# A bidirectional gated DeltaNet layer: the scan's ACT row is written anew, and the branch products between its steps are dealt out anew

## The chip, the cores and the metric

The kernel runs on one core of one Trainium2 chip. The metric is the device time of one execution in microseconds (us). The engines are named as in the profile: PE (TensorE, the matrix products), PEld (its weight loads), DVE (VectorE), ACT (ScalarE), POOL (GpSimd) and SP (SyncE, here only an issuer of DMAs). Each engine works through its own instructions strictly in order.

## The reference

One layer works on 2048 latent tokens and 256 context tokens of width 1024. It projects the normalised input, then runs two branches: A, a gated DeltaNet scan in both directions with eight heads of width 128, and B, a gated short convolution. Each branch is projected, gated, added, projected again, and a residual LayerNorm ends it. What matters here is the scan of branch A, cut to its core:

```python
def _gdn_chunked(q, k, v, g, beta, s0):
    g_cum = jnp.cumsum(g.reshape(b, h, n, CHUNK), axis=-1)
    decay = jnp.exp(jnp.where(tri_incl, g_cum[..., :, None] - g_cum[..., None, :], -jnp.inf))
    m = jnp.where(tri_strict, jnp.einsum('bhncd,bhnsd->bhncs', k_beta, k) * decay, 0.0)
    t_inv = lax.linalg.triangular_solve(eye + m, eye, left_side=True, lower=True)
    qk = jnp.einsum('bhncd,bhnsd->bhncs', q, k) * decay
    ...
    def step(s, xs):
        v_new = u_i - jnp.einsum('bhck,bhkv->bhcv', w_i, s)
        o = jnp.einsum('bhck,bhkv->bhcv', q_dec_i, s) + jnp.einsum('bhcs,bhsv->bhcv', qk_i, v_new)
        s = s * d_i[..., None, None] + jnp.einsum('bhck,bhcv->bhkv', k_dec_i, v_new)
        return s, o
```

## The kernel before

Three stages follow each other: the projections (to about 1860 us of the span), the scan in the function `window` (to about 2960 us), and `final` with the output projection and LayerNorm.

The scan treats chunks of 128 tokens. There are 18 chunks and two directions, so 36 visits, the directions by turns. One turn of the loop `for i in range(-3, nv)` works on several visits at once: `v0` runs its state step, `v1` finishes the triangular inverse, `v2` gets its product of queries and keys and the first, serial part of its inverse, and `v3` gets its decays and its product of keys and keys. The order of the lines in the loop is the order of each engine's row (`manual_schedule`). Nothing reorders it, so an instruction that waits holds all that stand behind it on its engine.

The names are these. `gcb` holds the decays: DVE forms eight differences (L143), ACT takes the exponential (L146), DVE multiplies by beta (L150). `gram` is the product on PE (L168) that becomes `N` (keys by keys) or `QK` (queries by keys) by a DVE product with `gcb` (L173). On a chunk's first visit ACT also copies the raw product to a tile (L171) and writes it to memory (L172, `kkd` for N and `kqd` for QK), and DVE's product waits for that copy. On the second visit, from the other direction, the raw product is loaded and only multiplied (L162). The first visits of the 16 latent chunks are called the first half here and their second visits the second half.

The inverse begins with `inv_base`, a generator that the loop advances with `go(sol, n)`. Four ACT copies take N's diagonal blocks (L182, `n32`), one more halves them (L186, `n16`), then DVE runs 15 row steps (`L200`, `L207`, `L210`: a shuffle into `rb`, a product and an addition into `R`), ACT spreads the result (L214, `r32`) and DVE transposes it (L217, `r32t`). The small products of `inv_w16` (L229, copied by ACT at L232) and `inv_d16` (L241, taken up by DVE at L243 and L245), and their like for 32 and 64 rows (L269, L283 to L285, L296 with the ACT copy `w64` at L299, L310) double the inverse's blocks. The large result `R` is laid out by ACT at L303 and completed at L311.

The state step is `st_ks` (PE L322, DVE L324), `st_v` (PE L331, ACT copy L334), `st_o` (PE L342 and L343) and `st_u` (PE L350, DVE L355). POOL scales keys (`kt`, L119) and queries (`qd`, L148).

Between these steps `dense(n)` puts n products of 128x512 of the branch projections on PE (L1286, L1288, L1290; "fillers" below). 24 of them make one tile, which DVE takes up at L1229 (`gt`). What the scan does not take runs at the head of `final`. The norms of finished chunks (`norm`, ACT L1497 and L1507, a chain of twelve tiny DVE steps) run only in the second half. The raw-product tile is named `zat` and has two buffers, and `norm` uses the same two:

```python
            if v["latent"]:
                kc = self.g1.tile([P, 4, P], F32, name="zat", bufs=2)
                nc.scalar.copy(out=kc, in_=kk)
                nc.scalar.dma_start(keep[:, hs], kc)
            nc.vector.tensor_tensor(out=N[:, hs], in0=kk, in1=v["gcb"][:, hs], op=ALU.mult)
```

Of the kernel before, what the change touches and what calls it, by code (L numbers as in the profile page):

```python
# [15 lines left out]
P = 128  # L16
# [21 lines left out]
class Kern:  # L38
# [118 lines left out]
    def gram(self, v, name, rhs):  # L157
# [6 lines left out]
        for g in range(2):  # L164
            hs = slice(4 * g, 4 * g + 4)
            kk = self.pg.tile([P, 4, P], F32, name="gram")
            for h in range(4 * g, 4 * g + 4):
                nc.tensor.matmul(kk[:, h - 4 * g, :], kT[:, h, :], rhs[:, h, :], start=True, stop=True)  # L168
            if v["latent"]:
                kc = self.g1.tile([P, 4, P], F32, name="zat", bufs=2)  # L170
                nc.scalar.copy(out=kc, in_=kk)  # L171
                nc.scalar.dma_start(keep[:, hs], kc)  # L172
            nc.vector.tensor_tensor(out=N[:, hs], in0=kk, in1=v["gcb"][:, hs], op=ALU.mult)  # L173
# [117 lines left out]
    def inv_w64(self, v):  # L291
# [6 lines left out]
        with self.tc.high_priority(100):  # L298
            nc.scalar.copy(out=v["w64"][p2], in_=wp[p2])  # L299
        v["R"] = R = self.g2.tile([P, H, P], F32, name="R")  # L300
# [890 lines left out]
    def window(self, es, settle):  # L1191
# [153 lines left out]
        with tc.manual_schedule(engines={ET.PE, ET.DVE, ET.Activation, ET.Pool, ET.SP}):  # L1345
# [22 lines left out]
            for i in range(-3, nv):  # L1368
# [4 lines left out]
                if i < -1:  # L1373
                    dense(FILL(i) // 2)
# [6 lines left out]
                go(sol, 2)  # L1381
                go(norms)
                if v1:
                    self.visit_load2(v1)
                    self.inv_w16(v1)

                if v2 and v2["latent"]:
                    self.gram(v2, "QK", v2["qT"])
                if i == -1 or v2 and v2["again"] or not v2:
                    dense(8)  # L1390
# [8 lines left out]
                go(sol)  # L1399
# [3 lines left out]
                go(sol)  # L1403
# [4 lines left out]
                if i >= -1:  # L1408
                    dense(4)
# [5 lines left out]
                if v0:  # L1415
                    self.st_u(v0, 0)
                if v1:
# [14 lines left out]
                if i >= -1:  # L1432
# [9 lines left out]
                go(dec)  # L1442
                if i >= -1:
                    dense(8)
                if v1:
                    self.inv_w64(v1)
                go(norms)
                go(sol, 9)
                go(dec)
                if i < -1:  # L1450
                    dense(FILL(i) - FILL(i) // 2)

                if v3:
                    self.gram(v3, "N", v3["kT"])
                    sol = self.inv_base(v3)
                if i == -1 or v3 and v3["again"] or not v3:
                    dense(8)
                ship()
                if v1:
                    self.inv_d64(v1)  # L1460
                go(sol, 2)
                go(norms)
                if i == -1 or not v3 or not v3["again"]:
                    dense(8)
# [281 lines left out]
```

## Time and profile before

| what | value |
|---|---|
| time, median of 3 runs (lowest, highest) | 3278.37 us (3275.57, 3281.44) |
| the profiled execution: its time, its span | 3288.09 us, 3286.4 us |
| busy share of PE, DVE, ACT, POOL over the span | 90%, 67%, 46%, 43% |
| mean granted clock of TensorE | 0.952 |
| first share of the chain that ended last | DVE 19%, PE 9%, DMA 6% |

The shares are means over stages with different limits. In the projections PE is busy nearly throughout. In the scan no engine is, and what ends the waits there has to be read visit by visit.

### The profile page before, as it was taken

To read this page: it belongs to the slowest core of one execution; us is meant where nothing else is said; L and a number is where in the kernel's file an instruction comes from. 1 tells how busy PE (TensorE), PEld (TensorE's weight loads), DVE (VectorE), ACT (ScalarE), POOL (GpSimd) and SP (SyncE) were. 2 spreads that over 40 slices of the span, in tenths; PEclk is the share of its full clock that TensorE was granted. 3 is DMA by queue.
4 is the path that set the end of the run, shared out by engine and by line. 5 is a ranking of instruction groups with operands and counts; after the bars stand their busy time and mean duration, and the time that the engine had idled before them with its cause. 6 is when DMAs were issued, how large, how long until landed. Compare 5 with 4: busy or idle time off the path is not lost. (4 is left out here: it accounts for less than half of the span.)

```text
span 3286.4 us, 60301 instructions
## 1 busy us (share of the span) xinstructions
PE 2963.1 (90%) x22089; PEld 2436.8 (74%) x22089; DVE 2212.4 (67%) x5658; ACT 1517.6 (46%) x3405; POOL 1401.0 (43%) x1021
## 2 busy tenths in 40 slices
PE   7899899999998899999999778899998688887887
PEld 3678668888886777888888667788887577775676
DVE  7756746565656574565732268887889799966499
ACT  4664644333446645333334145555555556552121
POOL 3443447766567554666666111111111222225264
PEclk9999999999999999999999989999998788898999
DMA  5533763324565433222233565575676668677742
GB/s 209 150 103 100 230 207 106 93 84 127 175 190 160 118 95 87 77 78 87 87 114 103 205 235 200 213 264 213 248 265 228 233 223 299 204 235 247 252 140 100
DMA packets 405380, 557.23 MB, mean 170 GB/s; under 512 B 28244, under 2 KB 278613, under 8 KB 404060
## 3 DMA queue, kind: packets, MB, share of 16 engines
q1 hardware_dynamic: 382158, 520.77, 48.7%
q10 hardware_dynamic: 22926, 32.62, 2.7%
q8 instruction: 173, 2.83, 0.3%
q14 instruction: 123, 1.01, 0.1%
HBM read 391.66 MB, written 161.64 MB: 168 GB/s over the span
## 5 line engine op out<-in xcount | busy, mean ns | idle before, releaser
L785 PE MATMUL pd<-bh,ah 128*128 128x512 f32 x2240 | 890.9, 398 | 10.4 <-ACT u L805 5.8
L787 PE MATMUL pd<-bh,al 128*128 128x512 f32 x2240 | 879.3, 393 | 0.0
L786 PE MATMUL pd<-bl,ah 128*128 128x512 f32 x2240 | 878.7, 392 | 0.0
L369 POOL TENSOR_TENSOR al<-s,ah 128x512 fp32r<-128x512 f32 x348 | 478.5, 1379 | 468.6 <-ACT ah L368 396.0
L369 POOL TENSOR_TENSOR al<-raw,ah 128x512 fp32r<-128x512 f32 x260 | 370.8, 1430 | 323.4 <-ACT ah L368 291.2
L785 PEld LDWEIGHTS pd<-bh,ah 128*128 128x128 f32 x2240 | 424.5, 190 | 99.4 <-issue 6.6
L787 PEld LDWEIGHTS pd<-bh,al 128*128 128x128 f32 x2240 | 424.2, 189 | 91.0 <-POOL al L369 0.2
L786 PEld LDWEIGHTS pd<-bl,ah 128*128 128x128 f32 x2240 | 424.5, 190 | 85.4
L368 ACT CAST ah<-s 128x512 fp32r<-128x512 f32 x352 | 214.3, 618 | 290.2 <-PE pd L786 262.8
L119 POOL TENSOR_TENSOR kt<-kt,kd 128x1024 f32<-128x1024 f32 x36 | 71.1, 1976 | 522.4 <-DMA kt<-kd 356.6
L368 ACT CAST ah<-raw 128x512 fp32r<-128x512 f32 x264 | 162.3, 616 | 263.1 <-PE pd L786 171.6
L1286 PE MATMUL pf<-ah,wh 128*128 128x512 f32 x512 | 219.1, 428 | 48.5 <-DMA wh<-w_bhd 21.9
L771 DVE TENSOR_TENSOR s<-s,raw 128x512 f32<-128x512 f32 x80 | 109.4, 1368 | 220.1 <-POOL s L771 220.1
L1290 PE MATMUL pf<-ah,wl 128*128 128x512 f32 x512 | 221.4, 432 | 20.0 <-DMA wl<-w_ald 17.4
L1288 PE MATMUL pf<-al,wh 128*128 128x512 f32 x512 | 216.4, 423 | 0.6 <-POOL al L369 0.6
L148 POOL TENSOR_TENSOR qd<-qd,qT 128x1024 f32<-128x1024 f32 x32 | 75.8, 2368 | 244.5 <-ACT qd L139 173.8
L207 DVE TENSOR_TENSOR rb<-rb,R 128x120 f32<-128x120 f32 (+4 forms) x540 | 165.2, 306 | 14.2
L210 DVE TENSOR_TENSOR R<-R,rb 128x120 f32<-128x120 f32 (+4 forms) x540 | 159.7, 296 | 1.2
L1286 PEld LDWEIGHTS pf<-ah,wh 128*128 128x128 f32 x512 | 103.9, 203 | 73.6 <-issue 34.9
L1290 PEld LDWEIGHTS pf<-ah,wl 128*128 128x128 f32 x512 | 103.9, 203 | 48.1 <-DMA wl<-w_ald 22.9
L1047 ACT ACTIVATE t<-t 128x512 f32<-128x512 f32 (+1 forms) x112 | 67.2, 600 | 141.2 <-DVE t L1032 141.1
L342 PE MATMUL pst<-S,qd 128*128 128x128 f32 x512 | 105.4, 288 | 17.5 <-ACT v L334 9.6
(349 smaller groups left out, 5911.1 us busy)
## 6 DMA issues: line engine op xcount, KB each, us to landing
raw<-in_w_in SPq DMA_DIRECT2D x160, 512.0 KB, 3.8
kT<-kTd SPq DMA_DIRECT2D x36, 512.0 KB, 9.0
gcb<-gcd SPq DMA_DIRECT2D x36, 512.0 KB, 6.0
kt<-kd SPq DMA_DIRECT2D x36, 512.0 KB, 7.1
vh<-vd SPq DMA_DIRECT2D x36, 512.0 KB, 8.4
wh<-w_bhd SPq DMA_DIRECT2D x32, 512.0 KB, 4.2
wl<-w_bld SPq DMA_DIRECT2D x32, 512.0 KB, 5.6
qT<-qTd SPq DMA_DIRECT2D x32, 512.0 KB, 9.1
```

Of the source, the lines that this page charges most:

```text
L207: nc.vector.tensor_tensor(out=t, in0=t, in1=bc(R[:, :, j:j + 1], c.stop - c.start), op=ALU.mult)
L210: nc.vector.tensor_tensor(out=R[:, :, c], in0=R[:, :, c], in1=t, op=ALU.add)
L342: nc.tensor.matmul(po[:, j, :], v["qd"][:, h, :], S[:, h, :], start=True, stop=False)
L368: self.nc.scalar.copy(out=hi, in_=src)
L369: (eng or self.nc.gpsimd).tensor_tensor(out=lo, in0=src, in1=hi.bitcast(F32), op=ALU.subtract)
L771: eng.tensor_tensor(out=o, in0=a, in1=b, op=op)
L785: mm(ps, hi[:, k, :], bh, start=(first and k == 0), stop=False, skip_group_check=not first)
L786: mm(ps, hi[:, k, :], bl, start=False, stop=False, skip_group_check=not first)
L787: mm(ps, lo[:, k, :], bh, start=False, stop=(last and k == 3), skip_group_check=not first)
L1286: mm(ps, wh[:, k, :], ah, start=(k == 0), stop=False)
L1288: mm(ps, wh[:, k, :], al, start=False, stop=False)
L1290: mm(ps, wl[:, k, :], ah, start=False, stop=(k == KT - 1))
```

## The change

Four things are done, all in the scan. The raw-product tile gets a name of its own, `kc`, with three buffers. The part of `inv_w64` that lays out `R` becomes a function of its own, `inv_x64`, called after N's product. The steps of the decays and of the serial inverse move: the exponential L146 goes behind the `w64` copy, `n32` and `n16` go from the end of a turn to the next turn behind the copies of QK, and more row steps stand after the decays' differences. The fillers are dealt out anew: 24 a turn in the first half and 32 in the second as before, at other places; 24 instead of 40 in the turn i = -1; 32 instead of 40 in the last turns.

```diff
-                kc = self.g1.tile([P, 4, P], F32, name="zat", bufs=2)
+                kc = self.g1.tile([P, 4, P], F32, name="kc", bufs=3)
...
+
+    def inv_x64(self, v):
+        nc = self.nc
         v["R"] = R = self.g2.tile([P, H, P], F32, name="R")
...
-                go(sol, 2)
-                go(norms)
                 if v1:
                     self.visit_load2(v1)
                     self.inv_w16(v1)
+                go(norms)
...
-                if i == -1 or v2 and v2["again"] or not v2:
-                    dense(8)
+                if full:
+                    dense(3 if gram_q else 11)
                 ship()
                 go(sol, 2)
...
-                go(sol)
                 if v0:
                     self.st_v(v0, 0)
                     self.st_v(v0, 1)
-                go(sol)
+                go(sol, 2)
...
-                if i >= -1:
-                    dense(4)
+                if full:
+                    dense(3)
...
-                go(dec)
-                if i >= -1:
-                    dense(8)
+                if full:
+                    dense(8 if gram_n else 6)
                 if v1:
                     self.inv_w64(v1)
+                go(dec)
                 go(norms)
-                go(sol, 9)
+                go(sol, 3)
                 go(dec)
...
                 if v3:
                     self.gram(v3, "N", v3["kT"])
+                if full:
+                    dense(4 if gram_n else 8)
+                ship()
+                go(sol)
+                if v1:
+                    self.inv_x64(v1)
+                    self.inv_d64(v1)
+                go(sol)
+                go(norms)
+                if full and gram_n:
+                    dense(2)
+                if v3:
                     sol = self.inv_base(v3)
-                if i == -1 or v3 and v3["again"] or not v3:
-                    dense(8)
-                ship()
-                if v1:
-                    self.inv_d64(v1)
-                go(sol, 2)
-                go(norms)
-                if i == -1 or not v3 or not v3["again"]:
-                    dense(8)
```

In the changed kernel the line numbers behind L297 are three higher (L303 becomes L306, L324 becomes L327), and behind `window`'s loop seven.

ACT's row around the copies of N in a turn of the first half, before:

```order
L146 ACTIVATE gcb<-gcb 128x1024
L299 COPY w_19036<-pinv 64x512
L303 ACTIVATE R<-r_18854,m64l 128x8x64
L303 ACTIVATE R<-r_18854,m64h 128x8x64
L214 ACTIVATE r_19041<-R_18717,m16l 128x8x16
L214 ACTIVATE r_19041<-R_18717,m16h 128x8x16
L171 COPY zat<-gram 128x512
L172 DMA kkd_181<-zat 128x512
L171 COPY zat<-gram 128x512
L172 DMA kkd_181<-zat 128x512
L311 ACTIVATE R<-pinv 64x8x64
```

The same place of the changed kernel:

```order
L299 COPY w_18976<-pinv 64x512
L146 ACTIVATE gcb<-gcb 128x1024
L171 COPY kc<-gram 128x512
L172 DMA kkd_181<-kc 128x512
L171 COPY kc<-gram 128x512
L172 DMA kkd_181<-kc 128x512
L214 ACTIVATE r_19013<-R_18776,m16l 128x8x16
L214 ACTIVATE r_19013<-R_18776,m16h 128x8x16
L306 ACTIVATE R<-r_18784,m64l 128x8x64
L306 ACTIVATE R<-r_18784,m64h 128x8x64
L314 ACTIVATE R<-pinv 64x8x64
```

The `w64` copy now precedes the exponential, and N's two copies come directly behind the exponential, ahead of `r32` and of `R`.

ACT's row right behind that place, before, to the copies of `st_v`:

```order
L182 ACTIVATE n_19075<-N 32x256 x4
L186 ACTIVATE n_19080<-n_19075,m16l 128x128
L232 COPY w_19165<-pinv 128x256
L171 COPY zat<-gram 128x512
L172 DMA kqd_197<-zat 128x512
L171 COPY zat<-gram 128x512
L172 DMA kqd_197<-zat 128x512
L334 COPY v_19243<-pst 128x512
```

The same place of the changed kernel:

```order
L232 COPY w_19090<-pinv 128x256
L171 COPY kc<-gram 128x512
L172 DMA kqd_197<-kc 128x512
L171 COPY kc<-gram 128x512
L172 DMA kqd_197<-kc 128x512
L182 ACTIVATE n_19114<-N 32x256 x4
L186 ACTIVATE n_19119<-n_19114,m16l 128x128
L337 COPY v_19167<-pst 128x512
```

The diagonal blocks moved from ahead of the copies of `w16` and QK to behind them.

DVE's row of the same turn from the decays' eight differences on, before:

```order
L143 SCALAR_TENSOR_TENSOR gcb<-gcb,gc,mask_283 128x128 x8
L207 TENSOR_TENSOR rb<-rb,R_19939 128x16
L200 STREAM_SHUFFLE rb<-n_19896 128x8
L210 TENSOR_TENSOR R_19939<-R_19939,rb 128x8x2
L207 TENSOR_TENSOR rb<-rb,R_19939 128x8
L210 TENSOR_TENSOR R_19939<-R_19939,rb 128x8
L217 STREAM_TRANSPOSE r32t<-r_20263 128x256
L150 TENSOR_TENSOR gcb<-gcb,cc 128x1024
L173 TENSOR_TENSOR N<-gram,gcb 128x512 x2
L1229 SCALAR_TENSOR_TENSOR gt<-gt,pf 128x512
L324 SCALAR_TENSOR_TENSOR vh<-pst,ngam,vh 128x128 x8
L188 SCALAR_TENSOR_TENSOR n_20302<-n_20297,m16h,n_20302 128x128
```

The changed kernel's row from the last of the row steps on; between L143 and these rows stand the row steps of widths 40, 32, 24 and 16 and `gt` (L1232):

```order
L207 TENSOR_TENSOR rb<-rb,R_19982 128x8
L210 TENSOR_TENSOR R_19982<-R_19982,rb 128x8
L150 TENSOR_TENSOR gcb<-gcb,cc 128x1024
L173 TENSOR_TENSOR N<-gram,gcb 128x512 x2
L217 STREAM_TRANSPOSE r32t<-r_20225 128x256
L327 SCALAR_TENSOR_TENSOR vh<-pst,ngam,vh 128x128 x8
L173 TENSOR_TENSOR QK<-gram,gcb 128x512 x2
L243 SCALAR_TENSOR_TENSOR r_20225<-pinv,m16h,r_20225 128x8x16
L245 STREAM_TRANSPOSE r32t<-r_20225 128x256
L188 SCALAR_TENSOR_TENSOR n_20335<-n_20330,m16h,n_20335 128x128
L189 TENSOR_TENSOR n_20335<-n_20335,tri_279 128x128
```

Behind L143 stand five row steps and `gt` where two row steps stood, the transpose L217 comes behind N's products, and the serial part (L188 on) begins only behind QK's products and the transposes of `inv_d16`.

## Rows read from the trace of the kernel before

**Rows 1.** Stretches: busy us of PE, PEld, DVE, ACT, POOL; clock, DMA share, GB/s.
```profile
1963.00:2432.60 469.60, 425.20 (x6375) 377.67 (x6374) 386.32 (x1669) 268.12 (x558) 79.07 (x53) 0.96 0.63 230
...
2650.00:2871.60 221.60, 183.42 (x2516) 161.08 (x2515) 206.30 (x785) 129.67 (x364) 55.13 (x38) 0.88 0.72 246
...
2965.00:3105.00 140.00, 107.43 (x394) 79.09 (x392) 68.86 (x80) 26.61 (x46) 45.88 (x31) 0.89 0.77 254
```

**Rows 2.** The chain that ended last, whole span: start, length, what (us).
```profile
1965.73 2.19 DVE gcb L143 x8
...
2432.78 2.11 DVE gcb L143 x8
...
2871.80 2.11 DVE gcb L143 x8
```

**Rows 3.** The same chain, through visits of the first half from 2130 us.
```profile
2133.73 0.72 ACT gcb L146
...
2136.74 0.58 ACT r L214 x2
...
2137.97 0.33 ACTq L172
...
2138.34 0.59 ACT zat L171
2138.95 5.99 DMA kkd<-zat
...
2145.64 0.69 DVE QK L173
...
2164.72 0.43 PE pf L1286
```

**Rows 4.** Waits of DVE in the first half: total, times, longest (us).
```profile
DVE r32t L217 <- ACT r L214: 49.5, 17, 3.0
DVE QK L173 <- ACT zat L171: 18.5, 11, 2.4
```

**Rows 5.** DVE in order of time, one visit: start, us, what.
```profile
2137.73 1.18 DVE L150 TENSOR_TENSOR gcb<-gcb,cc 128x1024 f32<-128x1024 f32 x1
2139.02 1.29 DVE L173 TENSOR_TENSOR N<-gram,gcb 128x512 f32<-128x512 f32 x2
...
2141.14 2.16 DVE L324 SCALAR_TENSOR_TENSOR vh<-pst,ngam,vh 128x128 f32<-128x128 f32 x8 [0.23 <-PE pst L322]
...
2154.42 0.21 DVE L210 TENSOR_TENSOR R<-R,rb 128x48 f32<-128x48 f32 x1
...
2154.90 2.26 DVE L210 TENSOR_TENSOR R<-R,rb 128x40 f32<-128x40 f32 x1
```

**Rows 6.** One of ACT's groups by line, first half: busy us, mean ns | idle before.
```profile
L182 ACT ACTIVATE n<-N 32x256 f32<-32x256 f32 x68 | 28.2, 414 | 10.7 <-DVE N L173 7.8 <-DVE N L162 2.3
```

**Rows 7.** PE in order of time, the same visit: start, us, what.
```profile
2135.44 1.14 PE L310 MATMUL pinv<-r,w 64*64 64x64 f32 x16 [1.66 <-ACT w L299]
...
2141.92 0.75 PE L229 MATMUL pinv<-r32t,n 32*32 32x32 f32 x64
2142.60 2.05 PE L168 MATMUL gram<-qT,kT 128*128 128x128 f32 x16
```

**Rows 8.** POOL in order of time, first half.
```profile
2090.40 1.90 POOL L119 TENSOR_TENSOR kt<-kt,kd 128x1024 f32<-128x1024 f32 x1 [16.93 <-DMA kt<-kd]
...
2154.74 2.36 POOL L148 TENSOR_TENSOR qd<-qd,qT 128x1024 f32<-128x1024 f32 x1 [5.73 <-ACT qd L139]
```

**Rows 9.** SP's DMA issues in order of time, first half.
```profile
2081.22 0.32 SPq L363 DMA_DIRECT2D wh<-w_bhd  x1
```

**Rows 10.** A stretch of 1 us, first half (columns as in Rows 1).
```profile
2138.00:2139.00 1.00, 1.00 (x4) 0.79 (x3) 0.91 (x1) 0.58 (x1) 0.00 (x0) 0.50 0.37 45
```

**Rows 11.** PE in order of time, a visit of the second half.
```profile
2663.14 1.08 PE L241 MATMUL pinv<-r,w 32*32 32x32 f32 x64 [3.66 <-ACT w L232]
```

**Rows 12.** The chain through the second half: a filler at the full clock.
```profile
2669.84 0.23 PE pf L1286
```

More of the change, by code (lines that the diff above doesn't have):

```diff
@@ L1372, in window @@
                 self.early = i < -1
-                if i < -1:
+                full = i >= -1
+                gram_q, gram_n = v2 and not v2["again"], v3 and not v3["again"]
+                if not full:
                     dense(FILL(i) // 2)
@@ L1441, in window @@
                 go(sol, 2)
-                go(dec)
-                if i >= -1:
-                    dense(8)
+                if full:
+                    dense(8 if gram_n else 6)
                 if v1:
                     self.inv_w64(v1)
+                go(dec)
                 go(norms)
-                go(sol, 9)
+                go(sol, 3)
                 go(dec)
-                if i < -1:
+                if not full:
                     dense(FILL(i) - FILL(i) // 2)
@@ L1454, in window @@
                     self.gram(v3, "N", v3["kT"])
-                    sol = self.inv_base(v3)
-                if i == -1 or v3 and v3["again"] or not v3:
-                    dense(8)
-                ship()
-                if v1:
-                    self.inv_d64(v1)
-                go(sol, 2)
-                go(norms)
-                if i == -1 or not v3 or not v3["again"]:
-                    dense(8)
+                if full:
+                    dense(4 if gram_n else 8)
[4 more added lines that the diff above has]
+                    self.inv_d64(v1)
+                go(sol)
+                go(norms)
+                if full and gram_n:
+                    dense(2)
+                if v3:
+                    sol = self.inv_base(v3)
             ship()
```

## The prediction

> **What bounds the kernel now.** I read the stretches of the span first, to see which engine is nearest to full where. In the first half of the scan DVE is busy 386.3 of 469.6 us and PE 425.2; in an undisturbed piece of the second half DVE is busy 206.3 of 221.6 us, 93%, and PE 183.4 at a clock of 0.88 [rows 1]. So the second half is nearly DVE's own work, and the first has air in it. The visits' length comes from the chain of the whole span: the eight differences of the decays (L143) open every visit, at 1965.73, 2432.78 and 2871.80 us, with 17 visits in the first gap and 14 in the second [rows 2]. That is 467.05 / 17 = 27.5 us a visit in the first half and 439.02 / 14 = 31.4 us in the second.
>
> Then the chain inside one visit. From the differences it goes through ACT (exponential, layout of R, r32, two copies of N), and from the second copy's end at 2138.93 into the write of that copy, 5.99 us, whose end lets ACT copy QK's second half into the same buffer; DVE's product with QK starts only behind it, at 2145.64 [rows 3]. DVE's own waits say what that costs where DVE stands: 49.5 us for the transpose L217, which waits for ACT's r32, and 18.5 us for QK, over 17 visits [rows 4]. That is 2.91 + 1.09 = 4.0 us a visit. PE waits too, 1.66 us in this visit for the w64 copy [rows 7], but as a follower.
>
> **What goes away.** The w64 copy no longer stands behind the exponential, so PE's wait for it ends: the copy can run as soon as L296 is through, and this costs nothing since N's product and four fillers lie over it. At the transpose, DVE has more of its own to do before it comes there. From the start of the exponential (2133.73) to the end of r32 (2137.32) ACT took 3.59 us, with the w64 copy, 0.59, and R's layout inside; 3.59 - 0.72 - 0.59 - 0.58 = 1.70 us is the layout and the starts between [rows 3]. The copy and the layout go, two copies of N and two issues come, 2 x (0.59 + 0.33) = 1.84: 3.6 us if the layout is nearly all of the 1.70, 4.8 if it were little of it. DVE in that time has five row steps (three instructions of some 0.2 us [rows 5] that partly overlap, some 0.4 us a step) and gt, of the size of one of N's two products, some 0.65: 2.65 us. L150 (1.18) and N's products (1.29) [rows 5] make it 5.1 us. So r32 is ready 0.3 to 1.5 us early and the 2.91 us vanish. I take all of them. The row steps and gt are not new work, they come from other places in DVE's row.
>
> The write's wait: four copies a visit go through three buffers, so QK's second copy still waits for a write, now N's first. In my walk N's first copy ends at 1.7 us after the differences and its write is issued at 2.0. QK's second product ends on PE at about 8.3: L217 ends at 5.5, inv_w16 takes 0.75 and the QK product 2.05 [rows 7]. The write has 6.3 us; the measured one took 5.99 while weights and keys were loading [rows 3]. These loads now stand earlier: wh is issued as PE crosses from one tile of fillers to the next, before behind L310, now six fillers ahead of L296, in my walk about 4.4 us before the differences end. I take the write as hidden; the bound is 0 to 1.7 us a visit if it lands 8 us after issue.
>
> **What comes instead.** n32 now stands behind both copies of QK. QK's copies end at 8.9 us in my walk, DVE's second QK product at 9.6; between vh (L324, 2.16 [rows 5], ends at 7.6) and that, DVE loses 0.4 + 0.3 us to these copies. Then PE: three fillers at 0.23 [rows 12] behind the QK product put inv_d16 at 9.7, and DVE takes it up with 0.15 lost. Then n32: four copies at 0.414 [rows 6] and n16, 0.4, from 9.25 on, ready at 11.35; DVE is through with the two inv_d16 steps at 10.5 and waits 0.9. Sum of the new waits 1.75 us. Net 4.0 - 1.75 = 2.25 us a visit, and a visit of 25.2 us. PE must fit: it comes to L229 with 0.8 us to wait for L217, and has 425.2 / 17 x 0.96 = 24.0 us of work in a visit at the full clock [rows 1], so it fits, barely.
>
> First half: 17 x 2.25 = **38 us**.
>
> Second half: there is little wait on DVE to win, 221.6 - 206.3 = 15.3 us over 7 visits, 2.2 each, part of it the gaps between dependent tiny steps [rows 1]. PE's largest wait is 3.66 us for the w16 copy, which stood behind the diagonal blocks and eight norm products [rows 11]; now only four norm products stand ahead. But the transpose L217 moves back to about 7.4 us behind the differences: five row steps 2.0, the norm's twelve tiny steps at some 0.2 each, L150 1.2, N's product about the same, the transpose 0.4. PE waits there instead, ahead of inv_w16 (0.7), eleven fillers (2.5 at 0.23, 4.7 at 0.43 [rows 3, 12]) and inv_d16 (0.7), which reaches DVE at 11.3 to 13.5; DVE, with vh 2.16 and QK's product 1.2, is ready at 10.8. Both gains and losses are of this size. I take 0.3 us a visit for 14 visits: **4 us**, between -1.6 and +2.2 a visit.
>
> The ends: 16 fillers fewer in turn i = -1, and eight fewer in each of the last turns, about 16 of which are then left to the head of `final`. There 394 of them took 140 us [rows 1], 0.36 each, which is +5 us; the shorter turns give back about 16 x 0.23 at each end, of which I take half: -4. Together **+1 us**, between -4 and +6.
>
> Sum: -38 - 4 + 1 = -41 us on the profiled execution's 3288.1. The median lies 0.3% below that execution, so 3288.1 - 41 = 3247, times 3278.37 / 3288.09, is **3237 us**.
>
> **Where a rule speaks against it.** Row first: a row step (L210) of width 48 took 0.21 us, the next of width 40 2.26 us; it began 0.16 us behind POOL's qd product of 2.36 us and ended with it, while L324, which reads PSUM, keeps its 2.16 us for eight [rows 5, 8]. So POOL's kt product (1.90 us) costs DVE up to its whole length wherever it meets row steps. Before it mostly fell into the QK wait: it ran 9.2 us behind wh's issue [rows 8, 9]. Issued 4.4 us ahead of the differences' end, the same 9.2 us put it at 4.8, over N's products, L217 and vh, which it doesn't stretch; if it lands 2.5 us sooner, without the writes of N beside it, it meets the row steps ahead of L150. [...]
>
> **Rivals.**
> 1. *Nothing replaces the waits, or the second half follows too.* DVE's waits go without the 1.75: 17 x 4.0 = 68 us, and 1.1 us of the second half's 2.2 on top, 15 us: 3278 - 82 = 3196. Against it: n32 behind QK's copies is plain in ACT's row.
> 2. *The write's wait stays.* Three buffers for four copies; at 8 us a landing it costs 1.4 us a visit, 24 us: 3261. For it: 5.99 us measured. Against it: the loads no longer stand beside it. Of the same size is kt's product on the row steps with the clock unharmed: 17 x 1.85 = 31 us, 3268.
> [...]
> 4. *No change.* The waits only move: what L217 and QK lose, n32 and inv_d16 gain. It needs 4.0 us of new waits where I count 1.75: 3278.
>
> **Chances.** Forecast (3215 to 3255): 0.50. Rival 1 and what lies towards it: 0.13. Rival 2 with its like, the port's rule on kt among them (3255 to 3271): 0.15. Rival 4: 0.07. Rival 3: 0.15. What a measurement of this kernel can tell from no change is about 0.2%, 6.6 us. So faster 0.78, same 0.07, slower 0.15. The range that leaves out no more than 2 in 10 reaches from 3205, most of the way to rival 1, to 3285, inside rival 3; the forecast's own range is 3215 to 3255.
>
> **What would show it.** Right: no DVE wait of L217 for ACT and none of QK for a write in the first half; the visits between the differences at 25 to 25.5 us; a wait of DVE's L188 for ACT's n16 of about 0.9 us; kt's product beside N's products, L217 and vh. In the second half visits of 30 to 31 us, with PE's largest wait at L229 and no longer at the w16 copy. [...] The step I trust least is where kt lands, since it rests on one distance, 9.2 us, taken under other traffic.

## The result and the profile after

The changed kernel takes 3245.01 us (median of 3 runs, 3239.52 to 3247.89) against 3278.37: a ratio of 0.9895, with a 95% interval from 0.987 to 0.9921. The prediction said 3237, between 3205 and 3285. The profiled execution has a span of 3246.2 us against 3286.4, so 40.2 us less. The kernel before was profiled in an execution 9.7 us above its median, the changed kernel in one 2.9 us above; that is why the medians lie only 33.4 us apart.

Where they went can be read from the starts of L141, the small product just ahead of the differences, which has one start per visit. In the kernel before these were 1963.37 us for the fifth visit, 2432.62 seventeen visits later and 2871.64 at the last. (The prediction counted from L143, which in that fifth visit came 2.3 us later, since L141 itself took 2.37 us; hence 469.25 us here and 467.05 there.) In the timeline of DVE after:

```profile
1954.30 0.16 DVE L141 TENSOR_TENSOR kd<-kd,cc 128x8 f32<-128x8 f32 x1
...
2058.73 0.16 DVE L141 TENSOR_TENSOR kd<-kd,cc 128x8 f32<-128x8 f32 x1
...
2084.00 0.16 DVE L141 TENSOR_TENSOR kd<-kd,cc 128x8 f32<-128x8 f32 x1
...
2111.97 0.16 DVE L141 TENSOR_TENSOR kd<-kd,cc 128x8 f32<-128x8 f32 x1
...
2400.57 0.16 DVE L141 TENSOR_TENSOR kd<-kd,cc 128x8 f32<-128x8 f32 x1
...
2835.62 0.16 DVE L141 TENSOR_TENSOR kd<-kd,cc 128x8 f32<-128x8 f32 x1
```

So 9.1 us were gained ahead of the fifth visit, 23.0 in the seventeen visits of the first half (446.27 us against 469.25, 26.25 a visit against 27.60), 4.0 in the fourteen of the second half (435.05 against 439.02), and 4.2 behind them. The prediction had 38, 4 and, for both ends together, a loss of 1.

The first half's visits are of two kinds: six take 25.0 to 25.3 us, as the one from 2058.73, and four 27.8 to 28.1, as the one from 2084.00; the rest lie between, or near the ends of the stretch. The stretches that answer to [rows 1], with the same columns:

```profile
1954.00:2400.60 446.60, 411.07 (x6308) 364.80 (x6308) 387.34 (x1670) 265.16 (x554) 83.53 (x51) 0.97 0.69 249
2614.30:2835.60 221.30, 181.73 (x2518) 156.86 (x2516) 191.95 (x787) 129.81 (x364) 54.66 (x38) 0.88 0.72 247
```

In the second half DVE is no longer busy 93% of the stretch but 87%, and yet the stretch is no shorter: the time went into a wait. The waits of the first half, DVE and then PE (engine, what waited, for what: total, times, longest):

```profile
DVE QK L173 <- ACT kc L171: 23.5, 32, 1.8
DVE n L188 <- ACT n L186: 16.2, 16, 1.1
...
PE pinv L229 <- DVE r32t L217: 32.1, 17, 5.4
```

The wait of L217 for `r32` (49.5 us, [rows 4]) is gone, and so is every wait for the write of `kkd`. In their place stand QK's wait for its own copy and L188's for `n16`.

The timeline in two visits: first POOL, DVE and PE in the fast visit from 2058.73, then SP's issue of `wh`, POOL's product on `kt`, DVE and PE in the slow visit from 2084.00:

```profile
2063.59 2.83 POOL L119 TENSOR_TENSOR kt<-kt,kd 128x1024 f32<-128x1024 f32 x1 [6.61 <-DVE R L210]
...
2063.45 1.22 DVE L150 TENSOR_TENSOR gcb<-gcb,cc 128x1024 f32<-128x1024 f32 x1
...
2066.55 0.74 PE L229 MATMUL pinv<-r32t,n 32*32 32x32 f32 x64 [0.91 <-DVE r32t L217]
2067.22 2.05 PE L168 MATMUL gram<-qT,kT 128*128 128x128 f32 x16
...
2081.56 0.32 SPq L366 DMA_DIRECT2D wh<-w_bhd  x1
...
2088.52 1.90 POOL L119 TENSOR_TENSOR kt<-kt,kd 128x1024 f32<-128x1024 f32 x1 [6.54 <-DVE R L210]
...
2088.64 1.81 DVE L210 TENSOR_TENSOR R<-R,rb 128x8 f32<-128x8 f32 x1
2090.36 1.21 DVE L150 TENSOR_TENSOR gcb<-gcb,cc 128x1024 f32<-128x1024 f32 x1
...
2096.99 0.69 DVE L173 TENSOR_TENSOR QK<-gram,gcb 128x512 f32<-128x512 f32 x1 [1.63 <-ACT kc L171]
...
2093.47 0.86 PE L229 MATMUL pinv<-r32t,n 32*32 32x32 f32 x64 [2.81 <-DVE r32t L217]
2094.26 3.49 PE L168 MATMUL gram<-qT,kT 128*128 128x128 f32 x16
```

In the slow visit `kt`'s product began 0.12 us ahead of the last row step, which took 1.81 us and not 0.17. L150 came 1.6 us later, L217 behind it, and PE waited 2.81 us ahead of L229. Behind that wait the QK product took 3.49 us and not 2.05, and DVE waited 1.63 us for the copy of it. In the fast visit L150 had begun 0.14 us before POOL came; then POOL was the one held, 2.83 us in place of 1.90, and nothing on DVE moved. The clock in two stretches of 1 us behind L229, one of the slow visit and one of the fast (columns as in [rows 1]; the clock is the third number from the end):

```profile
2094.00:2095.00 1.00, 1.00 (x27) 0.94 (x18) 1.00 (x5) 0.37 (x1) 0.00 (x0) 0.50 0.00 0
...
2067.00:2068.00 1.00, 1.00 (x39) 0.96 (x29) 1.00 (x5) 0.37 (x1) 0.00 (x0) 1.00 0.00 0
```

So two things make this visit long: DVE's stretched step and the clock. Two other visits of the first half show one without the other, that from 2320.78 (26.76 us) and that from 2191.28 (26.34 us):

```profile
2325.49 1.90 POOL L119 TENSOR_TENSOR kt<-kt,kd 128x1024 f32<-128x1024 f32 x1 [6.47 <-DVE rb L207]
...
2325.51 2.96 DVE L150 TENSOR_TENSOR gcb<-gcb,cc 128x1024 f32<-128x1024 f32 x1
...
2330.36 0.74 PE L229 MATMUL pinv<-r32t,n 32*32 32x32 f32 x64 [2.68 <-DVE r32t L217]
2331.03 2.05 PE L168 MATMUL gram<-qT,kT 128*128 128x128 f32 x16
...
2199.11 0.75 PE L229 MATMUL pinv<-r32t,n 32*32 32x32 f32 x64 [2.01 <-DVE r32t L217]
2199.79 3.63 PE L168 MATMUL gram<-qT,kT 128*128 128x128 f32 x16
```

In the first of them `kt`'s product came 0.02 us ahead of L150 and stretched it by 1.74 us. PE waited 2.68 us, the clock stayed at 1.00, and DVE waited 0.94 us in all for QK's copies, as in the fast visits. In the second nothing ahead of L217 was stretched; PE waited 2.01 us, the clock fell to 0.50, and DVE waited 2.38 us for QK's copies. Against the 25.0 to 25.3 us of the fast visits that makes, as an estimate, some 1.7 us a visit for a stretched step (26.76 us) and some 1.3 us for the clock of 0.50 (26.34 us). The four visits of 27.8 to 28.1 us have both. The length of PE's wait alone does not tell whether the clock falls.

Second half: the waits of PE and DVE over the stretch of seven visits, and then one visit in order of time.

```profile
PE pinv L229 <- DVE r32t L217: 35.3, 7, 6.4
...
DVE r L243 <- PE pinv L241: 15.4, 7, 3.8
```

```profile
2654.47 1.08 PE L229 MATMUL pinv<-r32t,n 32*32 32x32 f32 x64 [4.95 <-DVE r32t L217]
2655.47 0.80 PE L1289 MATMUL pf<-ah,wh 128*128 128x512 f32 x1
...
2660.46 0.76 PE L241 MATMUL pinv<-r,w 32*32 32x32 f32 x64
...
2661.27 0.35 DVE L243 SCALAR_TENSOR_TENSOR r<-pinv,m16l,r 128x128 f32<-128x128 f32 x1 [3.78 <-PE pinv L241]
```

PE waits 4.95 us for the transpose, its fillers behind that start 0.43 us apart at a granted clock of 0.50 (2655.50 to 2660.40), so that the eleven take nearly 5 us to L241, and DVE waits 3.78 us for them.

### The profile page after: what moved, and what is told of

The parts are those of the page before. It is cut to its first block, busy times and chain, and to the rows that moved or that the text cites. A ratio compares the mean times of both kernels' runs of the same rounds, so it can differ in the third digit from the quotient of the medians.

```text
span 3246.2 us, 60374 instructions
## 1 busy us (share of the span) xinstructions
PE 2952.5 (91%) x22089; PEld 2418.1 (74%) x22089; DVE 2192.1 (68%) x5662; ACT 1517.4 (47%) x3405; POOL 1405.8 (43%) x1017
## 3 DMA queue, kind: packets, MB, share of 16 engines
q8 instruction: 173, 2.83, 0.4%
## 5 line engine op out<-in xcount | busy, mean ns | idle before, releaser
L1289 PE MATMUL pf<-ah,wh 128*128 128x512 f32 x512 | 230.8, 451 | 39.8 <-DMA wh<-w_bhd 16.9
L774 DVE TENSOR_TENSOR s<-s,raw 128x512 f32<-128x512 f32 x80 | 116.2, 1452 | 217.4 <-POOL s L774 217.3
L1291 PE MATMUL pf<-al,wh 128*128 128x512 f32 x512 | 226.3, 442 | 0.6 <-POOL al L372 0.6
L1289 PEld LDWEIGHTS pf<-ah,wh 128*128 128x128 f32 x512 | 108.2, 211 | 64.5 <-issue 21.2
L210 DVE TENSOR_TENSOR R<-R,rb 128x120 f32<-128x120 f32 (+4 forms) x540 | 139.6, 258 | 1.2
L1291 PEld LDWEIGHTS pf<-al,wh 128*128 128x128 f32 x512 | 108.6, 212 | 21.5 <-POOL al L372 1.4
```

Source lines behind the costliest of these rows:

```text
L210: nc.vector.tensor_tensor(out=R[:, :, c], in0=R[:, :, c], in1=t, op=ALU.add)
L774: eng.tensor_tensor(out=o, in0=a, in1=b, op=op)
L1289: mm(ps, wh[:, k, :], ah, start=(k == 0), stop=False)
L1291: mm(ps, wh[:, k, :], al, start=False, stop=False)
```

## The experiments

The ratios are all to the kernel before on the same chip, as the changed kernel's 0.9895; a difference between two of them, times 3278 us, gives the microseconds between two kernels. "First half" and "second half" are the lengths between the same three starts of L141 as above. They come from one profiled execution of each kernel, which need not lie at its median: it took 13.6 us more in e10, 9.6 more in e8, 5.6 less in e3, 5.3 less in e4 and 4.9 less in e6 and e11. e5 leaves the first sixteen visits of the first half as they are, and there they are 2.3 us longer than in the changed kernel. So differences of 2 or 3 us in these columns say nothing.

| run | ratio (95% interval) | first half, us | second half, us |
|---|---|---|---|
| before | 1 | 469.3 | 439.0 |
| changed | 0.9895 (0.987 to 0.9921) | 446.3 | 435.1 |
| e1 | 0.9976 (0.9963 to 0.9989) | 462.5 | 432.5 |
| e2 | 0.9837 (0.9816 to 0.9858) | 431.2 | 430.0 |
| e3 | 0.9887 (0.9862 to 0.9912) | 445.0 | 422.6 |
| e4 | 0.9787 (0.9763 to 0.9812) | 419.9 | 426.5 |
| e5 | 0.9855 (0.9836 to 0.9875) | 449.9 | 428.9 |
| e6 | 0.984 (0.9821 to 0.9858) | 439.0 | 424.2 |
| e7 | 0.9825 (0.9804 to 0.9846) | 423.7 | 433.0 |
| e8 | 0.9881 (0.9859 to 0.9903) | 447.0 | 436.8 |
| e9 | 0.9811 (0.9796 to 0.9826) | 417.3 | 435.5 |
| e10 | 0.9868 (0.9852 to 0.9885) | 425.2 | 456.6 |
| e11 | 0.9858 (0.9843 to 0.9873) | 448.4 | 420.5 |
| e12 | 0.9777 (0.9757 to 0.9797) | 419.3 | 428.7 |

**e1, the buffer alone.** The kernel before with one line changed:

```diff
-                kc = self.g1.tile([P, 4, P], F32, name="zat", bufs=2)
+                kc = self.g1.tile([P, 4, P], F32, name="kc", bufs=3)
```

> The kernel before with nothing changed but the raw copies' own tile of three buffers. Theory A (the gain comes from several waits that each go for their own reason; the buffer is worth QK's wait for the write alone): DVE's wait of QK (L173), 18.5 us in 17 visits, goes, r32's wait (L217, 49.5 us) stays; the time is 3278 - 18 = 3260 us, visits of the first half at 26.5. Theory B (the buffer makes most of the gain, the order of ACT's row little): 3245 to 3250 us. Theory C (the wait only moves on to the next one on DVE): 3275 to 3280 us.

8 us faster: 3275.11 us, where the kernel before took 3281.62 on the same chip. On the scale of the expectations that is 0.9976 x 3278 = 3270 us, between A and C. QK's wait is gone from DVE's list, L217's is unchanged at 49.5 us, and the first half gained 6.8 us of the 18.5. DVE's waits and its stretch in the first half:

```profile
DVE r32t L217 <- ACT r L214: 49.5, 17, 3.0
```

```profile
1967.60:2430.10 462.50, 425.38 (x6303) 379.81 (x6303) 393.85 (x1666) 267.56 (x553) 76.73 (x51) 0.94 0.65 233
```

DVE is busy 7.8 us longer than before (386.0 in the same visits) though it does the same: `kt`'s product, which in the kernel before stretched row steps in eleven of the seventeen visits, in four of them by less than 0.6 us, now does so in sixteen, by 0.8 us or more. That is C's way for more than half of the amount.

**e2, `kt`'s product behind N.** Of the changed kernel, in `visit_load2`, which gets the visit behind (`w`):

```diff
+        if w:
+            nc.gpsimd.tensor_copy(out=self.kg, in_=w["N"][:, 7, 127:128])
         nc.gpsimd.tensor_tensor(out=kt, in0=kt, in1=bc(v["kd8"].unsqueeze(2), P), op=ALU.mult)
```

> The changed kernel; ahead of its product on kt, POOL copies one element of N's second half to a tile of its own, so that the product can't start before DVE has formed N. Theory A (the long visits of the first half, 27.8 to 28.1 us, come from kt's product on the row steps ahead of L150): the four long visits go down to 25.0 to 25.3, L150 starts 4.7 us behind L141 in every visit, 4 x 2.9 + 1.7 for the one visit in which the product stretched L150 = 13 us less, 3232 us. Theory B (the long visits come from PE's wait and its clock, whatever kt does): they stay, 3245 us. Theory C (kt's product behind N delays DVE's transpose L217 or vh instead): all visits at 26.5 to 27, 3250 to 3260 us.

Theory A. 3228.62 us; of the four long visits three take 25.0 to 25.3 us, and the fourth 26.8, behind a wait of 3.71 us ahead of L229 with the clock at 0.50 after it. Eleven of seventeen take 24.9 to 25.3 us, and the first half is 15.1 us shorter. DVE and POOL in the visit from 2106.13 (line numbers three higher again: L176 is N's product, L220 the transpose, L330 `vh`):

```profile
2112.17 1.29 DVE L176 TENSOR_TENSOR N<-gram,gcb 128x512 f32<-128x512 f32 x2
2113.38 0.43 DVE L220 STREAM_TRANSPOSE r32t<-r 128x256 f32<-128x256 f32 x1
2113.73 2.12 DVE L330 SCALAR_TENSOR_TENSOR vh<-pst,ngam,vh 128x128 f32<-128x128 f32 x8
...
2113.73 1.90 POOL L122 TENSOR_TENSOR kt<-kt,kd 128x1024 f32<-128x1024 f32 x1
```

The product lies over `vh` for its whole length, and neither is longer for it.

**e3, the fillers of the start put back.**

```diff
-                if full:
-                    dense(3 if gram_q else 11)
+                if full or not v2:
+                    dense(8 if i <= -1 else 3 if gram_q else 11)
...
-                    dense(4 if gram_n else 8)
+                    dense(8 if i == -1 else 4 if gram_n else 8)
...
-                if full and gram_n:
-                    dense(2)
+                if gram_n:
+                    dense(9 if i == -1 else 2 if full else 8)
```

> The changed kernel with the 40 fillers that it no longer has in the turns i = -3, -2 and -1 (16, 8 and 16) put back there. Theory A (the 9.1 us that the change gained ahead of the fifth visit are these 40 fillers at 0.23 us, and they cost nothing where they went): 3245 + 9 = 3254 us, with L141 of the fifth visit 9 us later. Theory B (they are paid for again at the head of the last stage, at 0.36 us): 3245 + 9 - 14 = 3240 us.

The same time as the changed kernel, 3244.97 us, so neither A's sum nor B's place. The fifth visit's L141 comes 8.4 us later, as both theories say, and most of that is given back in two visits of the second half. The fillers alone, ahead of the fifth visit and in these two visits, first in the changed kernel, then in e3 (busy us of PE, PEld and DVE, each with its count, then the clock and DMA columns of [rows 1]):

```profile
1866.00:1954.30 88.30, 46.34 (x159) 30.36 (x157) 4.10 (x6) 0.92 0.61 216
2512.28:2542.61 30.33, 10.54 (x33) 6.98 (x33) 0.68 (x1) 0.89 0.63 226
2542.61:2571.81 29.20, 7.37 (x20) 5.04 (x20) 1.36 (x2) 0.88 0.54 188
```

```profile
1866.00:1962.68 96.68, 51.26 (x190) 34.14 (x188) 5.43 (x8) 0.93 0.71 260
2517.75:2545.12 27.37, 3.38 (x10) 1.91 (x8) 0.69 (x1) 0.88 0.62 202
2545.12:2570.97 25.85, 0.00 (x0) 0.00 (x0) 0.00 (x0) 0.74 0.57 192
```

In these visits the fillers run out, since the next products of branch A need chunks that the scan has not finished. What is left out early is done there, 53 in place of 10, and the two visits are 6.3 us longer. (The first stretch shows 31 fillers more and not 40, since nine of the 40 stand ahead of 1866 us.)

**e4, `qd`'s product too.** As e2, and POOL's product on `qd` taken out of `visit_decay` and issued behind `kt`'s in the next turn:

```diff
-        if v["latent"]:
-            nc.gpsimd.tensor_tensor(out=qd, in0=qd, in1=v["qT"], op=ALU.mult)
         yield
...
+                if v2:
+                    self.visit_qd(v2)
                 go(norms)
```

> The changed kernel; kt's product stands behind N as in the run before, and POOL's product on qd, which lies on a row step in every visit (2.2 us), stands behind kt's in the next turn. Theory A (DVE's rows set the visits, and POOL's two products lie free over N's, vh's and QK's products, which read PSUM): PE with 411 us in 17 visits becomes the bound at 24.2 us, so 0.8 us a visit less in the first half on top of the 13 us of kt, 3232 - 14 = 3218 us, and up to 2.2 us a visit in 14 visits of the second half, down to 3187 us. Theory B (in the first half PE's wait at L229 takes the place of all of it and the second half, whose loop goes over L229 and inv_d16, gains nothing): 3232 us. Theory C (kt's and qd's products, 4.3 us one behind the other, meet QK's product or the second half's product of two SBUF tiles, L162): slower than 3245 us.

Theory A for the first half, 3212.22 us: it is 11.3 us shorter than e2's, where A has 14. Eleven of its seventeen visits take 23.9 to 24.4 us, and neither product stretches a row step any more. The second half gained only 3.5 us on e2. PE is the bound there, 405.94 of 419.8 us at a clock of 1.00 (columns as in [rows 1]):

```profile
1947.10:2366.90 419.80, 405.94 (x6326) 357.89 (x6325) 350.46 (x1666) 264.82 (x555) 78.89 (x68) 1.00 0.75 264
```

DVE's busy time is 36.9 us below the changed kernel's for the same instructions (350.46 against 387.34): that is how much of it I put down to POOL's two products.

**e5, fillers ahead of L229 in the second half.**

```diff
+                soon = 6 if full and not gram_q else 0
+                dense(soon)
                 if v1:
                     self.visit_load2(v1)
...
-                    dense(3 if gram_q else 11)
+                    dense((3 if gram_q else 11) - soon)
```

> The changed kernel; in the turns without a fresh QK (the second half) 6 of the 11 fillers that stand between inv_w16 and inv_d16 stand ahead of inv_w16, where PE waits for DVE's transpose (61.9 us at L229 in 13 visits), so that inv_d16 comes to DVE 1.4 to 2.6 us sooner. Theory A (in the second half the loop goes from the transpose L217 over PE's small product and the eleven fillers to inv_d16, for which DVE waits 28.1 us in 13 visits): up to 2.2 us a visit in 14 visits, 3245 - 25 = 3220 us. Theory B (DVE's own work is the bound there, its waits only move to the next product): 3240 to 3248 us. Theory C (the copy w16, which now has five fillers for cover and not eleven, makes PE wait): 3250 us.

3236.52 us. The second half is 6.2 us shorter in the profile, a quarter of what A says, and the intervals of the two kernels overlap; by the ratios it is 13 us faster; I count it as inconclusive.

**e6, the exponential ahead of the `w64` copy again.**

```diff
+                go(dec)
                 if full:
                     dense(8 if gram_n else 6)
                 if v1:
                     self.inv_w64(v1)
-                go(dec)
```

> The changed kernel with the exponential's place put back ahead of the w64 copy in ACT's row; all else as in the changed kernel. Theory A (the w64 copy's wait was only a follower and cost nothing, what freed the transpose L217 is the move of N's diagonal blocks and of R's layout): 3245 us, the w64 wait back on PE, visits of the first half still at 25 and 28. Theory B (the w64 copy ahead of the exponential is a part of the gain, since PE has 24.2 us of work in a visit of 26.2 and its wait of 1.7 us doesn't fit): 3255 to 3270 us.

Neither: 3228.77 us, 18 us faster than the changed kernel, 7.3 us of it in the first half and 10.8 in the second. The waits of PE, then of DVE, over the same seven visits of the second half as above:

```profile
PE pinv L313 <- ACT w L299: 18.1, 7, 4.1
PE pinv L229 <- DVE r32t L217: 6.3, 5, 2.3
...
DVE r L243 <- PE pinv L241: 6.8, 7, 2.1
```

The wait for the `w64` copy is back, and the one at L229 has fallen from 35.3 us to 6.3. PE waits less in sum, and it waits less right ahead of the loop to L241. DVE's wait at L243 falls from 15.4 to 6.8 us, and the seven visits are 9.4 us shorter. One visit:

```profile
2641.59 0.74 PE L229 MATMUL pinv<-r32t,n 32*32 32x32 f32 x64 [1.34 <-DVE r32t L217]
...
2642.61 0.39 PE L1291 MATMUL pf<-al,wh 128*128 128x512 f32 x1
...
2644.99 0.75 PE L241 MATMUL pinv<-r,w 32*32 32x32 f32 x64
```

From L229 to L241 it is 3.4 us here and 6.0 in the row of the changed kernel, with the fillers 0.23 us apart.

**e7, N's diagonal blocks at the turn's end.**

```diff
                 ship()
-                go(sol, 2)
                 if v1:
                     self.inv_d16(v1)
...
                 if v3:
                     sol = self.inv_base(v3)
+                go(sol, 2)
             ship()
```

> The changed kernel with N's diagonal blocks (n32, n16) put at the turn's end, behind inv_d64's copy and ahead of both QK copies in ACT's row, where the kernel before had them behind N's copies. Theory A (DVE's wait at L188, 16.2 us in 17 visits, is replaced by the same wait at QK's product, since four copies and n16, 2.1 us, then stand ahead of QK's copies): 3245 us. Theory B (ACT is idle at that place until PE has QK's product, so N's blocks cost nothing there): the wait at L188 goes, 16 us less, 3229 us. Theory C (the blocks push QK's copies by more than the wait that they save): 3255 us.

Theory B, and more: 3225.83 us. L188's wait is off the list, QK's is 27.1 us against 23.5, and the first half is 22.5 us shorter, with ten visits of 24.0 to 24.6 us. The waits account for 12.6 us of that at most. The rest comes with DVE's busy time, 372.0 us against 387.3 for the same work: POOL's products fall elsewhere, `qd`'s stretches a row step in eleven visits where it did in sixteen, and `kt`'s in two where it did in four. So this run changes two things at once.

**e8, the raw copies in the norms' buffers again** (e1's line the other way round).

> The changed kernel with the raw copies back in the norms' two buffers. Theory A (without the third buffer QK's copies wait for the writes of N, as in the kernel before, and the new order of ACT's row hides none of it): DVE's wait at QK grows by 1.1 to 1.8 us a visit, 3245 + 17 x 1.1 to 1.8 = 3264 to 3276 us. Theory B (the writes are hidden in the new order, since QK's copies come later behind N's): 3245 us. In the kernel before, the third buffer alone brought 8 us.

Theory B: 3242.44 us, the same as the changed kernel; no wait for a write of N is on the list.

**e9, three moves together**: e4, e6 and e7. **e10, a fourth**: e5 on top of e9.

> The changed kernel with kt's and qd's products behind N (33 us less in their own run), N's diagonal blocks at the turn's end (23 us less) and the exponential ahead of the w64 copy (18 us less). Theory A (each takes away another wait, and PE's own work of about 24.1 us a visit is the floor of the first half, where the first of them stands already): the first half stays at 24.1 us a visit, the second half gains the 11 us of the exponential and some of the blocks', 3208 - 15 = 3193 us. Theory B (the three add up): 3245 - 74 = 3171 us. Theory C (they take away the same wait, so that one is enough): 3208 to 3212 us.

> As the run of three moves, and in the second half 6 of the 11 fillers ahead of inv_w16, which brought 8 us by itself. Theory A (PE's wait at L229 is mostly gone with the exponential's place, so that the fillers there only delay inv_w16): the same as the run of three moves within 5 us. Theory B (the fillers still cover a wait): 8 us less than it.

e9 takes 3215.5 us, by the ratios 8 us more than e4, but the two intervals overlap: nothing gained on e4, which is C in size, and A in the first half. There PE is busy 97% of the time, and one visit after the other takes 23.97 us:

```profile
1976.90:2366.80 389.90, 379.77 (x5943) 338.04 (x5944) 327.40 (x1568) 250.36 (x522) 74.31 (x64) 0.99 0.75 263
```

The second half is 9 us longer than e4's. DVE's row steps wait 21.3 us there, and 12.6 in e4, for POOL's copy that starts R16. That copy stands behind `kt`'s product, which waits for its load. In e10 the same wait is 67.7 us, in a profiled execution 13.6 us above the median, and both theories missed: 3236.09 us, 19 us slower than e9. Why the six fillers, which helped a little alone, lengthen that wait has not been tried.

**e11, `r32` and the transpose straight behind the row steps.**

```diff
-                go(sol, 3)
+                go(sol, 5)
                 go(dec)
...
-                go(sol)
                 if v1:
                     self.inv_x64(v1)
                     self.inv_d64(v1)
-                go(sol)
                 go(norms)
```

> The changed kernel with ACT's r32 and DVE's transpose L217 put straight behind the last row step, ahead of L150 and N's products, as in the kernel before; ACT's other moves stay. Theory A (the gain of the first half is that DVE has L150 and N's products, 2.5 us, to do while ACT makes r32): the wait at L217 comes back with 2.0 to 2.9 us a visit, 17 x 2.5 = 42 us in the first half, 3280 to 3290 us. Theory B (the gain comes from ACT's row alone, where N's blocks and R's layout no longer stand ahead of r32): the wait is 1.1 us a visit (two copies of 0.4 us and the starts), 3245 + 17 = 3262 us. Theory C (the transpose comes sooner, PE's wait at L229 goes and makes up for it): 3235 to 3250 us.

Theory C in the result, 3231.06 us (12 us faster than the changed kernel, somewhat more than C has, though the two intervals just overlap), and B in the wait: DVE waits at L217 for 0.9 us a visit, not 2.9.

```profile
DVE r32t L217 <- ACT r L214: 14.2, 16, 1.9
```

The first half is not told apart from the changed kernel's (2.1 us longer), the second is 14.6 us shorter: behind L217 DVE now has L150 and N's product to do while PE goes from L229 to L241, and its wait at L243, 28.1 us in 13 waits in the changed kernel, is 2.2 us in 7.

**e12, e4 and e11, and R16's copy ahead of `kt`'s product.** The edits of both, and, besides the element that `kt`'s product waits for (it is taken from `gcb` on a first visit), this:

```diff
-        nc.gpsimd.tensor_copy(out=R, in_=rows(self.i16))
...
+                    self.inv_r16(v3)
                     sol = self.inv_base(v3)
```

> The run with kt's and qd's products held back (ratio to the kernel before 0.9787) with two things more: r32 and the transpose L217 straight behind the last row step, as in the run before this, and POOL's copy that starts R16 at the turn's end, ahead of the product on kt, so that no row step waits for it (12.6 us in three waits of the second half). In the turns with a fresh N the product on kt waits for L150, else for N. Theory A (the second half gains what r32's place gave there, 15 us, and most of the 12.6 us; the first half has 24.1 us a visit of PE's own work and can't gain): 3208 - 15 - 10 = 3183 us. Theory B (with kt's and qd's products over other work of DVE the second half's loop is already PE's, and r32's place gives nothing): 3200 us. Theory C (in the first half the transpose's wait of 0.9 us a visit now stands on the path, since the visits are 24.1 us and not 26): 3208 + 15 - 25 = 3198 us.

3207.58 us, the fastest run of all, but not told apart from e4 by their intervals; of the theories B comes nearest, with C's 3198 us close by. C's mechanism does not show: the first half is as long as e4's. The wait for R16's copy is gone, and the second half is no shorter for it: PE now waits 40.2 us in 390 at `st_o` for DVE's sum of the two directions (21.0 us in the second half of e4), and DVE waits 21.2 us for `r32`, 12.2 of it at once.

```profile
PE pst L354 <- DVE ot L1336: 40.2, 13, 7.4
...
DVE r32t L226 <- ACT r L223: 21.2, 12, 12.2
```

What sets the second half then has not been tried.

## Why the prediction was right, and where it was not

**The waits that go.** Right. L217's wait and the write's wait are both off the list. For the first the prediction's cause was DVE's own work ahead of the transpose; ACT's way to `r32` it reckoned no shorter than before, with N's two copies in it. e11 puts L150 and N's products, half of DVE's own work in the prediction's count, behind the transpose again, and still the wait is 0.9 us a visit and not 2.9. So the later place of the transpose earns the last 0.9 us at most and costs up to 14.6 us in the second half. How the other 2.0 us are shared between ACT's row and the row steps and `gt`, which stay ahead of the transpose in e11, is not shown; in e11 `r32` also stands ahead of N's copies again.

**The waits that come.** L188's wait for `n16` was put at 0.9 us a visit and is 16.2 / 17 = 0.95. QK's copies were put at 0.7 and cost 23.5 / 17 = 1.4: 0.94 in the visits of 25.0 us, 2.2 to 2.4 where the clock is at 0.50 behind L229. Together with 0.15 for `inv_d16` the prediction had 1.75; measured it is some 2.7 with the small ones and one wait of 4.4 us for POOL's copy that starts R16. In e7 L188's wait goes and QK's grows by 0.2 us a visit, so most of L188's part need not have been paid.

**First half, 38 us predicted, 23 measured.** The term that failed is where `kt` lands, which the prediction called its least trusted step. In the slow visit shown `wh` was issued 4.7 us ahead of the differences' end, about as counted (4.4), but `kt`'s product began 7.0 us behind it, not 9.2. So it came to the last row steps and L150 and not over N's products, as the prediction's own other case had it (2.5 us sooner). Whether it hurt hung on 0.1 us: where it began 0.14 us behind L150's start it was long itself (2.83 us), where it began 0.02 us ahead of it L150 was (2.96 us). With the product held back (e2) the first half is 15.1 us shorter, which is what was missing, and most visits are 25.0 to 25.3 us where 25.2 was predicted. That match is in part luck. In e2 the new waits are some 2.5 us a visit and not 1.75, but DVE's own work is 0.55 us a visit shorter than in the kernel before, since there `kt`'s product had stretched row steps in eleven visits; the prediction had it mostly inside the QK wait and counted no gain for this. What can make the kernel slower (rival 3, given 0.15) did come in four of the seventeen visits: `kt`'s product on the row steps ahead of L150, a wait of 2.4 to 5.4 us ahead of L229, the clock at 0.50 behind it, 28 us a visit. In e3 the same code for `kt`, behind other fillers at the start, stretches no row step of the first half: where the product falls is hardly to be foreseen from one distance. The range of the prediction ends inside rival 3, at 3285. No run shows the time of that rival, nor a length of PE's wait from which the clock is at 0.50: in the visit from 2320.78 a stretch of 1.74 us and a wait of 2.68 us left it at 1.00, and in that from 2191.28 it was at 0.50 behind 2.01 us. The chances also name a port's rule on `kt`. No run shows a port; what the changed kernel shows is `kt`'s product lengthening a row step in four of the seventeen visits (1.78 to 1.92 us), L150 in one (2.96) and L188 in two (1.61 and 1.94; 0.31 to 0.40 else).

The reading of [rows 5] that L324 keeps its 2.16 us has no POOL product beside it: POOL was idle from 2129.8 to 2147.1 us. It is e2 that shows it, with `vh` at 2.12 us under `kt`'s product. Two slips in the sums change nothing: 68 + 15 is 83 and not 82 (rival 1), and with nearly all of the 1.70 us as layout ACT's time to `r32` would be 3.1 us and not 3.6.

**The write.** Right that it is hidden, and e8 shows that with two buffers it would be too. In the old order the third buffer is worth 8 us, in the new one nothing that can be measured.

**The `w64` copy.** The prediction said that PE's wait for it ends and that this costs nothing. The second part was wrong: with the exchange undone (e6) the kernel is 18 us faster. PE's idle time did not go away; in the second half it gathered at L229, ahead of the loop to L241 that DVE waits for.

**Second half, 4 us predicted, 4 measured, for the wrong reason.** The wait at L229, the fillers at 0.43 us and an `inv_d16` that comes 2.2 us late are as the prediction described them. But the second half also took in fillers from the start, 438 recorded against 404 before. With these put back (e3) it is 16 us shorter than before and not 4, in an execution 5.6 us below e3's median; 6.3 us of the difference lie in the two visits shown.

**The ends, +1 us predicted, -13 measured**: 9.1 and 5.0 gained ahead of the fifth visit and in the last turns, 0.8 lost in `final`. The prediction counted 16 fillers less in turn -1 and overlooked 24 in turns -3 and -2, where the old conditions `not v2` and `not v3["again"]` also hold: 40 x 0.23 = 9.2 us. And it let them be paid for in `final`, where 412 fillers in place of 395 cost next to nothing; they are paid for in the second half. So it was luck that the total came near: the gain was put 15 us too high in the first half and 14 too low at the ends.

## What to carry to other kernels

In this kernel GpSimd's product on `kt` had a good place, over `vh`, for which VectorE reads PSUM (1.90 and 2.12 us in e2, neither longer for it), and a bad one, just ahead of VectorE's products of two SBUF tiles (a row step of 0.17 us took 1.81, L150 with its 1.22 took 2.96). When only a load decides where such a product falls, a one-element copy can make it wait for the right VectorE result. Over the seventeen visits of the first half that brought 15.1 us for `kt`'s product and 11.3 more for `qd`'s. A wait that an engine must have somewhere should not stand ahead of the step that another engine waits for next: moving PE's wait brought 18 us here with no work saved (e6). When work is dealt out anew, count what every branch condition gives in the first and last turns, and follow where the work that is left out is done in the end.

## What the runs showed of the hardware

In the cases shown here `kt`'s product on POOL and DVE's products of two SBUF tiles lengthened each other, each time the one that began second. In the changed kernel a product of 128x8 (L210), 0.17 us else, took 1.81 us where it began 0.12 us behind `kt`'s product, and L150, 1.22 us else, took 2.96 where it began 0.02 us behind it. `kt`'s product took 2.08 to 2.87 us in the six visits of the first half in which it began 0.10 to 0.89 us behind the start of L150, and 1.90 or 1.91 in the other eleven. The transpose L217, which reads one SBUF tile, kept its 0.43 us under `kt`'s product in the fast visit (at 2065.97 us), N's two products their 1.29 (at 2064.77 us), and `vh`, which reads PSUM, took 2.12 in e2 against 2.16 with POOL idle [rows 5]. What I had not expected is the amount: with the two POOL products, 4.3 us of work a visit, held back behind N (e4), DVE was busy 36.9 us less in the first half (350.46 against 387.34), and the first half was 26 us shorter.

How the clock answered a wait of PE cannot be read off the wait's length alone. In the changed kernel it stood at 1.00 behind L229 after waits of 0.91 and 2.68 us, and at 0.50 after 2.01, 2.81 and 4.95 us. What else decides it has not been tried. Behind L229 it was at 0.50 in six of the seventeen visits of the first half, after waits of 2.01 to 5.43 us, and in twelve of the fourteen of the second half, after 3.18 to 7.63 us.
